# A decoder layer with product-key experts: expert numbers made on chip, sub keys in four loads, list ranks in two-byte numbers, V's gathers tied to chunks, two late loads moved

## The chip, the cores and the metric

One core of a Trainium2 chip runs the whole layer in one launch. TensorE (PE) multiplies, VectorE (DVE) and ScalarE (ACT) work on rows of numbers, GpSimd (POOL) and SyncE (SP) here mostly start transfers (DMAs). Each engine works through its own list of instructions in order, and waits at an instruction until what that needs is there. The metric is the time of one run on the device in microseconds (us), lower is better; times are given as the median of several runs.

## What is computed

A decoder layer on 256 tokens of width 2048 in float32, and a last rmsnorm: two kinds of attention side by side, attention into a memory, and then a layer of experts, in which the change lies (the attention parts are left out here):

```python
def peer_ffn(x, w_q, sub_keys, u_tab, v_tab):      # 8 heads, 128 keys, 16 of the best
    q = (x @ w_q).reshape(T, 8, 2, 128)
    s = einsum('thpd,hpkd->thpk', q, sub_keys)
    top_s, top_i = top_k(s, 16)                    # for each half of the key
    cand = top_s[:, :, 0, :, None] + top_s[:, :, 1, None, :]
    best_s, best_c = top_k(cand, 16)
    expert = ia * 128 + ib                         # one of 16384
    gate = softmax(best_s)
    a = einsum('td,ted->te', x, u_tab[expert])
    return einsum('te,ted->td', gate * gelu(a), v_tab[expert])
h = h + peer_ffn(rmsnorm(h), ...)
y = rmsnorm(h)
```

## The kernel before

PE multiplies in float32 split in two: ACT rounds a block of weights to `hi` (line 75), DVE forms `lo = raw - hi` (line 77), and PE multiplies both, `hi` by 512 columns (line 124) and `lo` by 256 (line 126). SP loads the weights in halves of 512 KB into `raw` (line 66), a ring of four buffers; `hi` and `lo` are rings of three. A wait or a tie ("pin") can be put on any instruction: `pin` fixes only the order on one engine, `behind(ins, n)` makes an instruction wait for the n-th last `lo` that was written, so that it comes "in step with the blocks". Within these ties a list scheduler sets the order of each engine's instructions when the kernel is built.

The expert layer (`peer`) goes through these stages:

- **Queries and sub keys** (about 528 to 600 us). 16 blocks of `w_pq` are multiplied; for each of eight heads a 128 KB piece of the sub keys (`sk`, line 763) is loaded by SP. `whole`, a 2 MB copy of the hidden state, is loaded by POOL (line 758). The choice of the best 16 then goes on in pieces on DVE.
- **U** (about 600 to 1390 us). 128 chunks of U, 1 MB each, are multiplied by all tokens; gelu of each goes to a hidden tile `hb`, one tile for eight chunks, 16 tiles in all (`hidden_tile`). A hidden tile has 258 columns for each chunk: 256 tokens, and two for the number of the expert. The numbers come from a table in HBM, one load for each tile on SP (line 846, `hb<-number`, 128 x 8 x 2 words). In this stage POOL scatters the gates one by one into a `table` (line 1090, 256 indirect DMAs); it is read back and multiplied in.
- **Lists.** Experts that some token chose are sorted into five classes; `lists(part)` is called for experts 0 to 83 of each column (part 0, during U) and 84 to 127 (part 1, when V begins). Its steps `flags`, `totals`, `ranks`, `offsets`, `place`, `spots` are called one at a time between blocks of weights. `totals` and `ranks` are PE products of a matrix of 0 and 1 (`f`) with a triangle (`before`) in float32; `tot`, a copy of the totals, sits in a buffer of the `raw` ring. Then POOL writes the chosen hidden rows, sorted, to HBM (`rows`, line 967).
- **V** (about 1390 to 1710 us). POOL gathers the rows of V that are on a list, 128 rows (1 MB) at a time, 88 times, into the same buffers as the hidden tiles (`fetch`, line 1141, `vrows<-V,index`); the index of a class is loaded ahead (line 1137). PE multiplies with the sorted rows (`listed`), line 1170. The first ten gathers are called one per chunk after part 0's rows are written. `run` calls units of V's work, and every second half block a step of the list of part 1.
- **End.** `v_phase` first loads `res` (hidden state, `fin<-hres`, 2 MB, line 1249) and `gain` (`fin<-norm_final`, 1 MB, line 1250), and `one` (lines 1273 and 1274) is a square root of one element of `gain` that brings ACT's table of square roots in before the last rmsnorm needs it.

Of the kernel before, what the change touches and what calls it, by code (L numbers as in the profile page):

```python
# [18 lines left out]
F32 = mybir.dt.float32  # L19
F32R = mybir.dt.float32r  # L20
U32 = mybir.dt.uint32
# [7 lines left out]
T = 256  # L29
# [24 lines left out]
class Layer:  # L54
    def __init__(self, tc, a):
        self.tc, self.nc, self.a = tc, tc.nc, a
        self.written = ([], [])
        self.spread = {}
        self.pace = []
        self.hold = None  # L60
        self.last_mm = None


# [643 lines left out]
    def peer(self):  # L707
        nc, tc, a = self.nc, self.tc, self.a
        with ExitStack() as es:
# [5 lines left out]
            token = ba.tile([128, 2], F32, name="token")  # L715
            nc.gpsimd.dma_start(token, a["token"])
            self.token = token
            self.listing = False
# [13 lines left out]
            with ExitStack() as e2:  # L732
# [14 lines left out]
                with tc.tile_pool(name="tk", bufs=1, reuse_waits="tile") as tk:  # L747
# [5 lines left out]
                    self.rstd_rows(self.rstd, self.rstd, "sc", 2)  # L753
                    i16 = self.i16 = self.iota[:, :16]
                    whole = tk.tile([128, KD, T], F32, name="whole")
                    for q in range(4):
# [4 lines left out]
                    for h in range(8):  # L761
                        sk = tk.tile([128, 2, 128], F32, tag="sk", name="sk", bufs=8)
                        nc.sync.dma_start(sk, a["subkeys"][:, 2 * h:2 * h + 2, :])
                        if 2 <= h < 6:
                            for _ in range(2):
                                self.hidden_tile(ba)
                        pq = []
                        for p2 in range(2):
                            q = tk.tile([128, T], F32, tag="q", name="q", bufs=16)
                            if (h, p2) == (7, 1):  # L770
                                p = self.whole_block(a["w_pq"][2 * h + p2], whole)
                                nc.scalar.activation(q, p, AF.Copy)
                                self.renew(whole)
                            else:
                                p = self.fm_block(a["w_pq"][2 * h + p2], self.x3)
                                self.join(p, q)
                            pq.append(q)
                            step(2 * h + p2)
                        for tb in range(2):
                            pieces += self.topk_pieces(h, tb, pq, sk)  # L780
# [7 lines left out]
                cl = self.cl = es.enter_context(tc.tile_pool(name="cl", bufs=1, reuse_waits="tile"))  # L788
                self.before = cl.tile([128, 128], F32, name="before")
                nc.gpsimd.dma_start(self.before, a["before"])  # L790
                self.count = cl.tile([128, 2, 128], F32, name="count")
# [9 lines left out]
                while c < 128:  # L801
# [22 lines left out]
                    if part == 1 and not late and len(self.sets) < 10:  # L824
                        self.fetch(len(self.sets))
                    if steps:
                        steps.pop(0)()
# [15 lines left out]
    def hidden_tile(self, pool):  # L843
        t = pool.tile([128, GROUP, W], F32, tag="hb", name="hb", bufs=8)
        g = len(self.buf)
        self.nc.sync.dma_start(t[:, :, T:].bitcast(U32), self.a["number"][:, g * GROUP:(g + 1) * GROUP, :])
        self.buf.append(t)
# [35 lines left out]
    def lists(self, part, pool, tag, bufs):  # L883
# [8 lines left out]
        c = self.count[:, :, lo:hi]  # L892
        f, ok = t("f", 5), t("ok", 4)
        where = cl.tile([128, n], U32, tag="where", name="where")
# [13 lines left out]
        def totals():  # L908
            p = pool.tile([128, 512], F32, tag=tag, name="ps_tot", bufs=bufs)
            for j in range(5):  # L910
                ins = nc.tensor.matmul(p[:n, j:j + 1], f[:, j, :], self.ones[:, :1], start=True, stop=True)
                if j == 0:
                    self.pin(ins, self.last_mm)
            tot = self.st.tile([128, 4 * W], F32, tag="raw", name="tot", bufs=RAW)
            got["tot"] = tot = tot[:, :640].rearrange("p (k e) -> p k e", k=5)
            self.pin(nc.vector.tensor_copy(tot[:n], p[:n, :5].unsqueeze(2).to_broadcast([n, 5, 128])))

        def ranks():
# [4 lines left out]
            for j in range(5):  # L923
                ins = nc.tensor.matmul(got["sum"][:, j:j + 1], tot[:n, j, :], self.ones[:n, :1], start=True, stop=True)
                if j == 0:
                    self.pin(ins, self.last_mm)
                nc.tensor.matmul(p[:, j, :], self.before, f[:, j, :], start=True, stop=False)  # L927
                nc.tensor.matmul(p[:, j, :], tot[:n, j, :], self.before[:n, :n], start=False, stop=True)  # L928

        def offsets():  # L930

            s = small[:, 0:5]
# [23 lines left out]
        def spots():  # L956
            x = f[:, 0]
            self.pin(v.tensor_scalar(x, q, limit, ROWS[part] - limit - base[ALL], op0=ALU.is_ge, op1=ALU.mult))
# [4 lines left out]

        steps = [flags, totals, ranks, offsets, place, spots]

# [165 lines left out]
    def fetch(self, i):  # L1131

        nc = self.nc
        part, cls, k = self.seq[i]
        if (part, cls) not in self.index:
            t = self.cl.tile([128, CAPS[part][cls]], U32, name="index%d%d" % (part, cls))
            ins = nc.gpsimd.dma_start(t.unsqueeze(2), self.listed(part, cls)[:, :, T:T + 1].bitcast(U32))  # L1137
            self.after(ins, part)
            self.index[part, cls] = t
        raw = self.homes[i].tile([128, GROUP * W], F32, tag="hb", name="vrows", bufs=8)[:, :D]  # L1140
# [6 lines left out]
    def v_phase(self):  # L1147
# [6 lines left out]
        with ExitStack() as es:  # L1154
# [5 lines left out]
            def bank(tb):  # L1160
                ps = es.enter_context(psum("vps%d" % tb))
                out.append([ps.tile([128, 512], F32, name="out%d%d" % (tb, q)) for q in range(4)])
# [59 lines left out]
            def run(upto, beside=[], steps=[], every=2):  # L1222


                while at[0] < self.ends[upto]:
# [8 lines left out]
                    for hf in range(2):  # L1234
                        for unit in units:
                            half(unit, hf)
                            turn[0] += 1
                            if turn[0] % every:
                                continue
# [8 lines left out]
            bank(0)  # L1248
            nc.gpsimd.dma_start(res, self.hres)
            nc.gpsimd.dma_start(gain, a["norm_final"].partition_broadcast(128))  # L1250
            with psum("cps") as cps:
# [10 lines left out]
                assert not steps  # L1262
            bank(1)
            run(1, late)

            for tb in range(2):
# [5 lines left out]
            one = vw.tile([128, 1], F32, tag="fy", name="one", bufs=2)  # L1272
            nc.scalar.activation(one, gain[:, :1], AF.Square)
            nc.scalar.activation(one, one, AF.Sqrt)
# [152 lines left out]
def arrays_of(x, mem, t5_table, norm_mix, w_in, cmp_pos_k, cmp_w1_k, cmp_w2_k, cmp_pos_v, cmp_w1_v,  # L1427
# [43 lines left out]
    r["before"] = (i[:, None] < i[None, :]).astype(f)  # L1471
    r["number"] = np.zeros((128, 128, W - T), np.uint32)
    r["number"][:, :, 0] = i[None, :] * 128 + i[:, None]
    r["order"] = (i[None, :] * 128 + i[:, None]).astype(f)
# [18 lines left out]
```

## Time and profile before

| | |
|---|---|
| runs | 1728.80, 1727.91, 1722.69 us; median 1727.91 us |
| the profiled execution | 1721.46 us, of which the span of instructions is 1719.7 us; mean granted clock of TensorE 0.982 |
| busy | PE 1646.6 us (96%), DVE 1260.7 (73%), ACT 1004.6 (58%), POOL 763.0 (44%) |
| moved | 419.08 MB in 137197 packets, 39273 of them under 512 B |
| largest groups | `lo` on DVE 534.7 us, `hi` on ACT 460.2 us, PE's products of line 124 585.5 us and of line 126 323.7 us |

PE is busy for 96% of the span. A busy PE is not PE at its peak: it counts as busy while a product runs at half clock too. So the count of products in a stretch, beside its busy time and its granted clock, says more than the share. PE's busy time by itself leaves 73.1 us of the span.

### The profile page before, as it was taken

How to read it: one execution, taken by the hardware profiler on the slowest of the kernel's cores; microseconds unless marked ns; L12 is line 12 of the kernel's file. 1: busy time of each engine (PE TensorE's matmuls, PEld its weight loads, DVE VectorE, ACT ScalarE, POOL GpSimd, SP SyncE). 2: the span in 40 equal slices, each digit the busy share in tenths (PEclk: the TensorE clock that was granted, in tenths of full speed). 3: DMA queues.
4: the chain of work that ended last, by engine and by line, in shares of the span. 5: the costliest groups of instructions: out<-in, count | busy, mean ns of one | idle time of the engine just before them, and what ended most of it. 6: DMA issues, size and time to landing. Idle time of an engine off the chain costs nothing. (4 is left out here: it accounts for less than half of the span.)

```text
span 1719.7 us, 25752 instructions
## 1 busy us (share of the span) xinstructions
PE 1646.6 (96%) x8808; PEld 1392.2 (81%) x8808; DVE 1260.7 (73%) x2260; ACT 1004.6 (58%) x1486; POOL 763.0 (44%) x652
## 2 busy tenths in 40 slices
PE   8999999999999999999999899999999989899996
PEld 6788777887888888888888688878788766677874
DVE  6875664556768888899999358787556469688687
ACT  7555556765566456566665356654455456567566
POOL 6510000212224376787888741102886216886620
PEclk9999999999999999999999899999999989999998
DMA  8668344889847666566656468766788956998991
GB/s 301 232 213 272 117 163 144 314 313 387 314 136 234 211 187 181 175 195 186 184 174 197 131 191 305 257 232 220 243 277 260 386 214 249 362 402 311 413 406 60
DMA packets 137197, 419.08 MB, mean 244 GB/s; under 512 B 39273, under 2 KB 52201, under 8 KB 123360
## 3 DMA queue, kind: packets, MB, share of 16 engines
q1 hardware_dynamic: 97424, 253.69, 45.5%
q0 software_dynamic: 39344, 163.13, 25.6%
q8 instruction: 71, 1.16, 0.3%
q14 instruction: 70, 0.57, 0.1%
q10 hardware_dynamic: 288, 0.52, 0.1%
HBM read 373.40 MB, written 51.75 MB: 247 GB/s over the span
## 5 line engine op out<-in xcount | busy, mean ns | idle before, releaser
L77 DVE TENSOR_TENSOR lo<-raw,hi 128x1024 fp32r<-128x1024 f32 x433 | 534.7, 1239 | 248.2 <-ACT hi L75 155.5
L75 ACT ACTIVATE hi<-raw 128x1024 fp32r<-128x1024 f32 x437 | 460.2, 1056 | 373.9 <-issue 127.2
L124 PE MATMUL acc<-pair_f,hi 128*128 128x512 f32 x2288 | 585.5, 398 | 14.9 <-ACT hi L75 9.8
L124 PEld LDWEIGHTS acc<-pair_f,hi 128*128 128x128 f32 x2288 | 416.1, 191 | 95.0 <-ACT hi L75 10.6
L1090 POOL DMA_INDIRECT table<-total,place x256 | 328.7, 1284 | 143.3 <-DVE lo L77 62.6
L126 PEld LDWEIGHTS acc<-pair_f,lo 128*128 128x128 f32 x2288 | 314.8, 192 | 33.8 <-issue 6.6
L126 PE MATMUL acc<-pair_f,lo 128*128 128x256 f32 x2288 | 323.7, 284 | 9.2 <-issue 5.6
L967 POOL DMA_INDIRECT rows<-hb,where x128 | 152.0, 1187 | 72.9 <-issue 35.0
L1141 POOL DMA_INDIRECT vrows<-V,index x88 | 124.0, 1410 | 77.3 <-DVE lo L77 21.7
L104 ACT ACTIVATE hi<-vrows,val 128x1024 fp32r<-128x1024 f32 x96 | 109.5, 1148 | 79.5 <-PE out L1170 42.4
L106 DVE SCALAR_TENSOR_TENSOR lo<-vrows,val,hi 128x1024 fp32r<-128x1024 f32 x96 | 123.0, 1283 | 40.2 <-ACT hi L104 32.6
L124 PE MATMUL acc<-pair_x,hi 128*128 128x512 f32 x512 | 132.4, 397 | 0.0
L77 DVE TENSOR_TENSOR lo<-vrows,hi 128x1024 fp32r<-128x1024 f32 x80 | 97.8, 1222 | 13.8 <-issue 4.7
L124 PEld LDWEIGHTS acc<-pair_x,hi 128*128 128x128 f32 x512 | 92.0, 190 | 16.6 <-issue 0.8
L75 ACT ACTIVATE hi<-vrows 128x1024 fp32r<-128x1024 f32 x80 | 84.1, 1052 | 21.4 <-PE out L1170 17.7
L1170 PE MATMUL out<-hi,hh 128*128 128x512 f32 x256 | 82.1, 411 | 14.7 <-ACT hi L75 5.9
L1170 PE MATMUL out<-hi,hl 128*128 128x512 f32 x256 | 82.4, 404 | 0.2
L1170 PE MATMUL out<-lo,hh 128*128 128x512 f32 x256 | 78.3, 407 | 0.6 <-DVE lo L77 0.4
L126 PE MATMUL acc<-pair_x,lo 128*128 128x256 f32 x512 | 75.1, 285 | 0.0
L126 PEld LDWEIGHTS acc<-pair_x,lo 128*128 128x128 f32 x512 | 70.9, 191 | 5.0
L1170 PEld LDWEIGHTS out<-hi,hh 128*128 128x128 f32 x256 | 47.0, 191 | 32.2 <-ACT hi L75 11.8
L124 PE MATMUL acc<-pair_o,hi 128*128 128x512 f32 x256 | 64.8, 394 | 3.8 <-ACT hi L75 2.9
(397 smaller groups left out, 2229.1 us busy)
## 6 DMA issues: line engine op xcount, KB each, us to landing
raw<-U SPq DMA_DIRECT2D x256, 512.0 KB
raw<-w_sb SPq DMA_DIRECT2D x32, 512.0 KB
table<-zero POOLq DMA_DIRECT2D x16, 1024.0 KB
raw<-w_out SPq DMA_DIRECT2D x32, 512.0 KB
raw<-w_pq SPq DMA_DIRECT2D x32, 512.0 KB
listed<-rows SPq DMA_DIRECT2D x88, 129.0 KB
rows<-zero POOLq DMA_DIRECT2D x12, 903.0 KB
gates<-table POOLq DMA_DIRECT2D x20, 512.0 KB
```

The source lines that it names most:

```text
L75: nc.scalar.activation(hi, raw, AF.Copy)
L77: self.last_lo = (eng or nc.vector).tensor_tensor(out=lo, in0=raw, in1=hi.bitcast(F32), op=ALU.subtract)
L104: nc.scalar.activation(hi, raw, AF.Copy, scale=val)
L106: self.last_lo = nc.vector.scalar_tensor_tensor(lo, raw, val, hi.bitcast(F32), op0=ALU.mult, op1=ALU.subtract)
L124: mm(ps, hi[:, n * m:(n + 1) * m], pair[:, k, :], start=first and n == 0, stop=False)
L126: self.last_mm = mm(ps[:, T:], lo[:, n * m:(n + 1) * m], pair[:, k, :T], start=False, stop=last and n == len(ks) - 1)
L967: ins = nc.gpsimd.indirect_dma_start(out=self.rows[part], out_offset=bass.IndirectOffsetOnAxis(ap=where[:, i - lo:i - lo + 1], axis=0), in ...
L1090: ins = self.nc.gpsimd.indirect_dma_start(out=self.table, out_offset=bass.IndirectOffsetOnAxis(ap=self.place[tb][:, s:s + 1], axis=0), in_ ...
L1141: self.gather = nc.gpsimd.indirect_dma_start(out=raw, out_offset=None, in_=self.a["V"], in_offset=bass.IndirectOffsetOnAxis(ap=self.index[ ...
L1170: self.last_mm = mm(out[tb][hf * 2 + q], h, v[:, q * 512:(q + 1) * 512], start=first and n == 0, stop=last and n == len(passes) - 1)
```

## The change

Six parts, of which the core of the diff follows.

1. `hidden_tile` no longer loads the numbers; DVE computes them from a row 0..7 (`iota`) and a small constant `base`, 128 x 16, loaded once.
2. The sub keys come in four loads of 256 KB on POOL's queue, ahead of `whole`, into one tile.
3. `f`, `before`, `tot` and the column of ones are two-byte numbers (BF16), which hold these whole numbers exactly; the five products of `f` with `before` become one of 420 (part 1: 220) columns; `tot` leaves the `raw` ring; `before` is loaded to a buffer of that ring first and cast.
4. `offsets` and `place` are one step, and the steps of part 1's list are called after each half block of V.
5. `fetch` loads the indices of up to three following gathers behind the last gather; each of the first ten gathers waits for the latest `lo` of its chunk.
6. `fin<-hres` is put behind the gathers that `run(0)` calls, `fin<-norm_final` behind those of `run(1)`; `one` goes to the place where it is written, near the end.

```diff
@@ peer
+            self.base = ba.tile([128, 16], F32, name="base")
+            nc.gpsimd.dma_start(self.base, a["base"])
...
+                    keys = tk.tile([128, 16, 128], F32, name="sk")
+                    for q in range(4):
+                        nc.gpsimd.dma_start(keys[:, q * 4:q * 4 + 4, :], a["subkeys"][:, q * 4:q * 4 + 4, :])
                     whole = tk.tile([128, KD, T], F32, name="whole")
...
-                        sk = tk.tile([128, 2, 128], F32, tag="sk", name="sk", bufs=8)
-                        nc.sync.dma_start(sk, a["subkeys"][:, 2 * h:2 * h + 2, :])
+                        sk = keys[:, 2 * h:2 * h + 2, :]
...
-                self.before = cl.tile([128, 128], F32, name="before")
-                nc.gpsimd.dma_start(self.before, a["before"])
+                self.before = cl.tile([128, 128], BF16, name="before")
+                wide = self.st.tile([128, 4 * W], F32, tag="raw", name="wide", bufs=RAW)[:, :128]
+                nc.gpsimd.dma_start(wide, a["before"])
+                self.pin(nc.vector.tensor_copy(self.before, wide))
...
                         self.fetch(len(self.sets))
+                        self.behind(self.gather, 1)
@@ hidden_tile
-        self.nc.sync.dma_start(t[:, :, T:].bitcast(U32), self.a["number"][:, g * GROUP:(g + 1) * GROUP, :])
+        self.pin(self.nc.vector.tensor_scalar(t[:, :, T:].bitcast(U32), self.iota[:, :GROUP].unsqueeze(2).to_broadcast([128, GROUP, W - T]),
+                                              128.0, self.base[:, g:g + 1], op0=ALU.mult, op1=ALU.add))
@@ lists
-            tot = self.st.tile([128, 4 * W], F32, tag="raw", name="tot", bufs=RAW)
+            got["tot"] = tot = wide[:, :320].bitcast(BF16).rearrange("p (k e) -> p k e", k=5)
...
             for j in range(5):
-                ins = nc.tensor.matmul(got["sum"][:, j:j + 1], tot[:n, j, :], self.ones[:n, :1], start=True, stop=True)
+                ins = nc.tensor.matmul(got["sum"][:, j:j + 1], tot[:n, j, :], self.unit[:n, :1], start=True, stop=True)
...
-                nc.tensor.matmul(p[:, j, :], self.before, f[:, j, :], start=True, stop=False)
-                nc.tensor.matmul(p[:, j, :], tot[:n, j, :], self.before[:n, :n], start=False, stop=True)
+            nc.tensor.matmul(p.rearrange("p k e -> p (k e)"), self.before, f.rearrange("p k e -> p (k e)"),
+                             start=True, stop=False)
+            for j in range(5):
+                nc.tensor.matmul(p[:, j, :], tot[:n, j, :], self.before[:n, :n], start=False, stop=j == 4)
...
-        steps = [flags, totals, ranks, offsets, place, spots]
+        steps = [flags, totals, ranks, lambda: (offsets(), place()), spots]
@@ v_phase
+                            if steps and every == 2:
+                                steps.pop(0)()
+                                continue
                             if turn[0] % every:
...
             bank(0)
-            nc.gpsimd.dma_start(res, self.hres)
-            nc.gpsimd.dma_start(gain, a["norm_final"].partition_broadcast(128))
...
             bank(1)
+            self.pin(nc.gpsimd.dma_start(res, self.hres), self.gather)
             run(1, late)
+            self.pin(nc.gpsimd.dma_start(gain, a["norm_final"].partition_broadcast(128)), self.gather)
...
-            nc.scalar.activation(one, gain[:, :1], AF.Square)
+            self.pin(nc.scalar.activation(one, gain[:, :1], AF.Square))
```

How the order of instructions stands, by engine. A row gives the line, the operation, what is written and read, the size, and how often in a row. First SP's queue, from the first weights of the query to the end of U, before the change (`sk` are sub keys, `hb<-number` the numbers of a hidden tile):

```order
L66 DMA raw<-w_pq 128x1024 x8
L763 DMA sk<-subkeys 128x256 x3
L846 DMA hb<-number 128x8x2 x2
L66 DMA raw<-w_pq 128x1024 x2
...
L846 DMA hb<-number 128x8x2 x2
L763 DMA sk<-subkeys 128x256 x2
L66 DMA raw<-w_pq 128x1024 x21
L66 DMA raw<-U 128x1024 x116
L846 DMA hb<-number 128x8x2 x8
L66 DMA raw<-U 128x1024 x140
```

and of the changed kernel, from the memory's weights to V's first sorted rows:

```order
L67 DMA raw<-w_mem_q 128x1024 x8
L67 DMA raw<-w_mem_o 128x1024 x8
L67 DMA raw<-w_pq 128x1024 x32
L67 DMA raw<-U 128x1024 x256
L1205 DMA listed<-rows_80 128x258 x19
```

Nothing is left between SP's loads of weights. Next the load of `before`. It stood on POOL ahead of all puts of gates (`table<-total,place`; `whole` is the copy of the hidden state):

```order
L716 DMA token<-token 128x2
L758 DMA whole<-hres 128x1024 x4
L790 DMA before<-before 128x128
L1090 DMA table<-total_4916,place_4918 4194304x1 x16
L1090 DMA table<-total_4917,place_4919 4194304x1 x16
```

It now goes to a buffer of the `raw` ring (`wide`), and on POOL it stands behind the first 194 of the 256 puts; the sub keys stand ahead of `whole`:

```order
L717 DMA token<-token 128x2
L719 DMA base<-base 128x16
L760 DMA sk<-subkeys 128x512 x4
L764 DMA whole<-hres 128x1024 x4
L1102 DMA table<-total_4916,place_4918 4194304x1 x16
...
L1102 DMA table<-total_4916,place_4918 4194304x1 x2
L796 DMA wide<-before 128x128
L1102 DMA table<-total_4916,place_4918 4194304x1 x14
```

and on DVE, among the pieces of the last choice of experts (`bs`, `bi`, `place`), the cast that reads it:

```order
L997 MAX bs<-cand 128x8
L78 TENSOR_TENSOR lo<-raw,hi 128x1024
L799 CAST unit<-ones 128x2
L797 CAST before<-wide 128x128
L1064 TENSOR_SCALAR place_4918<-key,token 128x16
L998 MAX_INDEX bi<-bs,cand 128x8
L1000 MATCH_REPLACE rest<-bs,cand 128x256
L1037 TENSOR_SCALAR bm<-bs 128x1
L78 TENSOR_TENSOR lo<-raw,hi 128x1024
```

The cast stands behind the 277th `lo<-raw,hi` of the kernel, counted in DVE's order; the last eight hidden tiles' numbers (line 856) are written on DVE behind the 290th and the 291st. Last ACT around `one`, before, among the first blocks of V (`hh` is the rounded part of the sorted rows):

```order
L104 ACTIVATE hi<-vrows,val 128x1024
L75 ACTIVATE hi<-vrows 128x1024
L1273 ACTIVATE one<-fin 128x1
L1274 ACT_TABLE_LOAD
L1274 ACTIVATE one<-one 128x1
L1177 ACTIVATE hh<-listed 128x128 x2
L104 ACTIVATE hi<-vrows,val 128x1024
```

and in the changed kernel, among the last blocks of V and the squares of the last rmsnorm (line 1300):

```order
L1300 ACTIVATE fin,z_17103<-out_14370 128x512
L1291 ACTIVATE one<-fin 128x1
L1192 ACTIVATE hh<-listed 128x128
L105 ACTIVATE hi<-vrows,val 128x1024
L76 ACTIVATE hi<-vrows 128x1024
L1292 ACT_TABLE_LOAD
L1292 ACTIVATE one<-one 128x1
L105 ACTIVATE hi<-vrows,val 128x1024
L1300 ACTIVATE fin,z_17103<-out_14371 128x512
```

The table of square roots is now loaded in the last stage instead of the first of V. On POOL, `fin<-hres` and `fin<-norm_final` stood right behind the tenth gather; now the first stands ahead of the twelve writes (line 979) that begin part 1's rows, and the second 70 rows behind it, past part 1's index loads. On DVE the last step of part 1's list (`where`) stands behind the same `lo` of V, the 23rd, in both kernels.

More of the change, by code (lines that the diff above doesn't have):

```diff
@@ L61, in __init__ @@
         self.last_mm = None
+        self.gather = None
     def raw(self, src):
@@ L788, in peer @@
                 cl = self.cl = es.enter_context(tc.tile_pool(name="cl", bufs=1, reuse_waits="tile"))
-                self.before = cl.tile([128, 128], F32, name="before")
-                nc.gpsimd.dma_start(self.before, a["before"])
+                self.before = cl.tile([128, 128], BF16, name="before")
+                wide = self.st.tile([128, 4 * W], F32, tag="raw", name="wide", bufs=RAW)[:, :128]
+                nc.gpsimd.dma_start(wide, a["before"])
+                self.pin(nc.vector.tensor_copy(self.before, wide))
+                self.unit = cl.tile([128, 2], BF16, name="unit")
+                self.pin(nc.vector.tensor_copy(self.unit, self.ones[:, :2]))
                 self.count = cl.tile([128, 2, 128], F32, name="count")
@@ L892, in lists @@
         c = self.count[:, :, lo:hi]
-        f, ok = t("f", 5), t("ok", 4)
+        f, x = cl.tile([128, 5, n], BF16, tag="f", name="f"), cl.tile([128, n], F32, tag="x", name="x")
+        wide = cl.tile([128, 336], F32, tag="ok", name="ok")
+        ok = wide[:, :4 * n].rearrange("p (k e) -> p k e", k=4)
         where = cl.tile([128, n], U32, tag="where", name="where")
@@ L910, in totals @@
             for j in range(5):
-                ins = nc.tensor.matmul(p[:n, j:j + 1], f[:, j, :], self.ones[:, :1], start=True, stop=True)
+                ins = nc.tensor.matmul(p[:n, j:j + 1], f[:, j, :], self.unit[:, :1], start=True, stop=True)
                 if j == 0:
                     self.pin(ins, self.last_mm)
-            tot = self.st.tile([128, 4 * W], F32, tag="raw", name="tot", bufs=RAW)
-            got["tot"] = tot = tot[:, :640].rearrange("p (k e) -> p k e", k=5)
+            got["tot"] = tot = wide[:, :320].bitcast(BF16).rearrange("p (k e) -> p k e", k=5)
             self.pin(nc.vector.tensor_copy(tot[:n], p[:n, :5].unsqueeze(2).to_broadcast([n, 5, 128])))
@@ L956, in spots @@
         def spots():
-            x = f[:, 0]
             self.pin(v.tensor_scalar(x, q, limit, ROWS[part] - limit - base[ALL], op0=ALU.is_ge, op1=ALU.mult))
@@ L1133, in fetch @@
         nc = self.nc
-        part, cls, k = self.seq[i]
[L1135 to L1139, printed above, removed]
+        for p, cls, _ in self.seq[i:i + 3]:
+            if (p, cls) not in self.index and p == self.seq[i][0]:
+                t = self.cl.tile([128, CAPS[p][cls]], U32, name="index%d%d" % (p, cls))
+                ins = nc.gpsimd.dma_start(t.unsqueeze(2), self.listed(p, cls)[:, :, T:T + 1].bitcast(U32))
+                self.after(ins, p)
+                if self.gather is not None:
+                    self.pin(ins, self.gather)
+                self.index[p, cls] = t
+        part, cls, k = self.seq[i]
         raw = self.homes[i].tile([128, GROUP * W], F32, tag="hb", name="vrows", bufs=8)[:, :D]
@@ L1471, in arrays_of @@
     r["before"] = (i[:, None] < i[None, :]).astype(f)
-    r["number"] = np.zeros((128, 128, W - T), np.uint32)
-    r["number"][:, :, 0] = i[None, :] * 128 + i[:, None]
+    r["base"] = (np.arange(16)[None, :] * (GROUP * 128) + i[:, None]).astype(f)
     r["order"] = (i[None, :] * 128 + i[:, None]).astype(f)
```

## The prediction

> **What bounds the kernel now.** The engine table comes first: PE is busy for nearly the whole span.
>
> ```profile
> PE 1646.6 (96%) x8808; PEld 1392.2 (81%) x8808; DVE 1260.7 (73%) x2260; ACT 1004.6 (58%) x1486; POOL 763.0 (44%) x652
> ```
>
> A stage can then only get shorter where PE does fewer products in a time than it can, or does products that go away. So the second view is PE's busy time by stretch, with the count of products; the stretches lie where the change touches the work, the first and the fifth where nothing disturbs U and V, the last inside the second.
>
> ```profile
> core 0: us, PE busy (x), PEclk, DMA share, GB/s
> 900.00:936.00 36.00, 36.00 (x208) 1.00 0.61 190
> 942.00:978.00 36.00, 27.67 (x118) 0.76 0.49 115
> 556.00:576.00 20.00, 16.53 (x91) 0.91 0.74 223
> 1348.00:1364.00 16.00, 12.49 (x63) 0.89 1.01 419
> 1612.00:1668.00 56.00, 56.00 (x242) 1.00 1.02 414
> 1389.00:1445.00 56.00, 45.39 (x176) 0.85 0.77 293
> 954.00:972.00 18.00, 9.67 (x27) 0.63 0.23 78
> ```
>
> An undisturbed product of U costs 36/208 = 0.173 us, one of V 56/242 = 0.231 us. 942 to 978 is 90 products short: 15.6 us. 556 to 576 should hold 116 and holds 91: 4.3 us. 1348 to 1364 should hold 92.5 and holds 63: 5.1 us. Of the 176 records at V's opening 40 belong to the lists, so 136 of 242 are V's: 24.5 us. That is what there is to win, 49.5 us; the rest of the kernel is at its rate.
>
> **The numbers of the experts.** SP's timeline at the hole in U, the transfers of 943 to 952, and one of PE's waits in 942 to 978:
>
> ```profile
> 941.03 7.71 SPq L846 DMA_DIRECT2D hb<-number  x8
> 948.84 35.04 SPq L66 DMA_DIRECT2D raw<-U  x10
> ```
>
> ```profile
> DMA packets 8594, 0.33 MB, mean 36 GB/s; under 512 B 8531, under 2 KB 8531, under 8 KB 8594
> ```
>
> ```profile
> PE acc L126 <- issue: 4.7, 6, 1.1
> ```
>
> The eight loads hold SP for 7.71 us, and their 8531 packets leave 36 GB/s, where U takes 190 GB/s. The loads go; on DVE eight small writes of 16 elements come, at some 0.2 us each (the smallest operation of ACT below takes 0.20), and 8 KB of `base`: 1.6 us, hidden by the microseconds that a `lo` lies ready before PE takes it up (4.2 us in the next part); without that cover it is 1.6 us. I take the whole 15.6 us. The lower end is little above 0: PE is slowest from 954 to 972, after the packets, and waits there for nothing that the profile shows (the issue row). The other eight loads and the sub keys lie between `w_pq` loads, and ACT waits for these (waits of 541 to 571):
>
> ```profile
> ACT hi L75 <- DMA raw<-w_pq: 8.3, 2, 6.4
> ```
>
> 4 us of 4.3. The sub keys, 1 MB, now go ahead of `whole` on POOL's queue: at 190 GB/s 5.5 us, behind which `whole` lands later; ACT scales `whole` one or two `hi` later than before, which covers about that. Bounds: 0 and 5.
>
> **The cast of `before`: a new wait.** The load stood before all puts; now it stands behind 194 of them, and DVE waits for it in its own order. Where DVE comes to it, where POOL then is, and where PE is (timelines; the first POOL row is an undisturbed put, the one of 917.78 the 195th, the last a gather that waits for a small load of POOL):
>
> ```profile
> 907.62 1.21 DVE L77 TENSOR_TENSOR lo<-raw,hi 128x1024 fp32r<-128x1024 f32 x1
> ...
> 910.86 2.03 DVE L1063 TENSOR_TENSOR dup<-place 128x1792 f32<-128x1792 uint32 x1
> ```
>
> ```profile
> 904.14 0.98 POOL L1090 DMA_INDIRECT table<-total,place  x1 [0.30 <-issue]
> ...
> 909.99 3.75 POOL L1090 DMA_INDIRECT table<-total,place  x1 [0.30 <-DVE bm L1025]
> 914.05 3.42 POOL L1090 DMA_INDIRECT table<-total,place  x1 [0.31 <-DMA table<-total,place]
> 917.78 1.23 POOL L1090 DMA_INDIRECT table<-total,place  x1 [0.30 <-issue]
> ...
> 1336.00 1.04 POOL L1141 DMA_INDIRECT vrows<-V,index  x1 [2.19 <-DMA index<-rows]
> ```
>
> ```profile
> 915.12 1.11 PE L126 MATMUL acc<-pair_f,lo 128*128 128x256 f32 x8
> ```
>
> The 277th `lo` is that of 907.62; it ends at 908.8, and there is the cast. POOL works without a pause, so the load is issued when the 194th put ends, at 917.5 by these rows; with some 2.5 us to its landing (estimate from the gather's wait of 2.19 us, which is the last part of such a landing) DVE stands still for 11 us. If the two long puts are long because of DVE's work beside them (`dup` lies inside the first), a still DVE lets them take 0.98 us: the load is issued at 912.3, and DVE waits 6 us. Behind the cast stand pieces of the choice and the next `lo`, which was done at 910.95 and which PE took up at 915.12, 4.2 us later; of the following eleven, counted in the same way, the closest has 1.9 us to spare, and DVE has no idle time before 940 in which to catch up. PE so loses 4 to 9 us, and up to 1.7 more by half clock: ends 4 and 11. I take 6, since the long puts stand just where DVE is busy. The Trainium skill ("SBUF — State Buffer", Who interferes with whom) speaks against that: it infers that DVE's tensor_tensor, which `dup` is, does not keep POOL from writing descriptors. By it the puts stay long, the cast costs 9 to 11, and the sum below is 4 us higher; the row of 3.75 us lies beside `dup` and so leans against it, without proof.
>
> **The ranks.** PE's groups of part 0's ranks, and the first and last of part 1's 30 records:
>
> ```profile
> L927 PE MATMUL ps_rank<-f,before 128*128 128x84 f32 x10 | 2.2, 297 | 0.0
> L928 PE MATMUL ps_rank<-before,tot 84*128 84x84 f32 x10 | 1.9, 275 | 0.0
> L924 PE MATMUL ps_rank<-ones,tot 84*128 84x1 f32 x10 | 1.6, 224 | 0.0
> ```
>
> ```profile
> 1408.78 0.38 PE L924 MATMUL ps_rank<-ones,tot 44*128 44x1 f32 x2
> ...
> 1413.15 0.65 PE L928 MATMUL ps_rank<-before,tot 44*128 44x44 f32 x2
> ```
>
> Each product in float32 is two passes. Part 1: 30 records from 1408.78 to 1413.8, 5.0 us (0.165 each), now ten of one pass and a wide one (0.3, estimate from 297 ns for 84 columns of these): 2.0, so 3.0 us saved. Part 0, whose 30 records are busy for 5.7 us and overlap to 3.3: by the same shares 2.0 saved, and half a microsecond more for both totals: 5.5. Bounds 0 (a pass in two bytes could cost what two cost) and 8 (all of it).
>
> **The burst of gathers.** Transfers of 1338 to 1348, by queue (POOL's, then SP's):
>
> ```profile
> q0 software_dynamic: 401, 2.92, 70.0%
> q1 hardware_dynamic: 350, 1.29, 31.9%
> ```
>
> U gets 1.29 MB in 10 us, 129 GB/s. One gather for each chunk takes 3.6 us at POOL's 292 GB/s, in a chunk of 5.55 us (32 products); U moves 0.46 MB beside it and 0.8 MB in the rest at 414 GB/s, where it needs 1.05. So the burst's loss goes: 4.5 of 5.1 (0 to 5.1).
>
> **V's opening.** ACT, PE's next product, and one behind a later wait; then two stretches at half clock:
>
> ```profile
> 1400.75 0.20 ACT L1273 ACTIVATE one<-fin 128x1 f32<-128x1 f32 x1 [3.67 <-DMA fin<-norm_final]
> 1400.97 1.28 ACT L1274 ACT_TABLE_LOAD   x1
> ```
>
> ```profile
> 1402.71 1.22 PE L1170 MATMUL out<-hi,hh 128*128 128x512 f32 x2 [3.91 <-ACT hh L1177]
> ```
>
> ```profile
> 1439.84 0.63 PE L1170 MATMUL out<-hi,hh 128*128 128x512 f32 x1 [2.57 <-DVE total L951]
> ```
>
> ```profile
> 1412.70:1419.50 6.80, 6.80 (x18) 0.50 0.92 329
> 1440.00:1443.40 3.40, 3.40 (x9) 0.50 1.02 421
> ```
>
> ACT waits in order for `gain`, then loads the table, and `hh` is behind both: 3.91 us, and 1.7 for the half clock after it. With part 1's ranks cut to 2 us I let the 6.8 us at half clock behind them go as well (3.4). With 5.6 and 3.4 this is 9.0. The clock also halves after 2.57 us of waiting (the stretch at 1440, which stays, behind `place`). The Trainium skill ("TensorE: Matmul & The Clock Gate", Part 1: The HAM clock gate) halves it only after an idle window of about 3.4 us; by that rule the 6.8 us, with no gap ahead of them, have a cause that the change leaves, and the sum is 3.4 us higher; the row of 1440 speaks against the rule.
>
> Costs: `offsets` with `place` in one step puts about 1 us more of DVE work ahead of a `lo` that PE waits for at 1437; the table load of 1.28 us comes where ACT has no idle time (row below): 1.3 us. `hres` and `gain`, 3 MB, move to stretches of V; at 414 GB/s 7.3 us of transfers, hidden by the gathers' lead if that holds, else up to 2 us a megabyte. Earlier calls of the list's steps gain nothing: `where` stands behind the same `lo`.
>
> ```profile
> 1690.00:1700.00 10.00, 10.00 (x17) 1.00 0.01 2
> ```
>
> **Sum.** 15.6 + 4 + 5.5 + 4.5 + 9.0 = 38.6 gained, 6 + 1 + 1.3 = 8.3 lost: 30.3 us. 1721.5 (the profiled run) becomes 1691.2. The three runs have their median 6.4 above that run; I add half of it: 1694.
>
> **Rivals.**
> 1. The slow stretch of 954 to 972 has another cause than the loads and stays. There 27 products stand where 104 fit: 13.3 us not won, 1707. For it: its waits have no releaser, and the packets are over by 953. Against: U's own transfers stand at 78 GB/s there, so its chain of buffers is broken as well.
> 2. The tied gathers starve U all the same: at 129 GB/s a chunk takes 8.1 us instead of 5.55, ten chunks 26 us, 1720. Against: each gather is alone in its chunk.
> 3. The clock rule above: 1698.
> 4. Slower: the wait at the cast grows, DVE standing for POOL's queue. PE's loss is the wait less 1.9 us, so from 38.6 - 2.3 + 1.9 = 38 us on nothing is gained, and at 55 us it is 1727.9 + 17 = 1745. POOL would have to be at its 194th put at 945 instead of 917; it is late by 9 us now, and puts go on to 1014.
>
> **Chances.** Forecast 0.58, rival 1 0.18, 2 0.09, 3 0.09, 4 0.03, and 0.03 for what I don't see. The range takes the cast's ends (1692 to 1700), rival 1 and a better case without the 3.2 us of median, the burst and the table in full (1683): 1682 to 1710; rival 2 and 4 are left out. Within 0.5% (8.6 us, about what a measurement of this kernel tells from no change) is 1719 to 1737, most of it rival 2's upper half: 0.06; slower 0.04; faster 0.9.
>
> **What would show it.** After: no thin stretch behind the 290th `lo`, PE at 208 products in 36 us there; DVE idle 6 to 11 us ahead of a cast of `before` that waits for its load, with a PE gap of some us behind it; no `hb<-number`; ten gathers 5.5 us apart and no gap of PE at 1354; V's first 56 us with about 60 more products; ranks in about 2 us. The prediction is wrong if the thin stretch stays, if a gather delays `hi`, or if DVE stands over 12 us at the cast.

## The result, and the profile after

The changed kernel takes 1714.82 us (median; 1702.78 to 1721.1), the kernel before 1728.3 us beside it: ratio 0.9924, interval 0.9903 to 0.9945. That is faster by 13.5 us, where 34 were forecast; 1714.8 lies above the range of 1682 to 1710. The profiled execution took 1713.96 us, span 1711.9, 7.8 us less than the span before.

The engine table after, and PE's busy time in stretches (columns: from and to, length, PE busy and its instructions, granted clock, DMA share, GB/s):

```profile
PE 1635.5 (96%) x8760; PEld 1378.7 (81%) x8760; DVE 1264.4 (74%) x2278; ACT 1004.4 (59%) x1486; POOL 756.9 (44%) x657
```

```profile
core 0: us, PE busy (x), PEclk, DMA share, GB/s
900.00:936.00 36.00, 33.25 (x187) 1.00 0.62 192
942.00:978.00 36.00, 34.40 (x197) 1.00 0.63 177
970.00:990.00 20.00, 13.65 (x58) 0.84 0.32 89
1208.00:1240.00 32.00, 23.48 (x99) 0.89 0.57 177
...
1382.00:1438.00 56.00, 43.92 (x177) 0.91 0.76 283
1612.00:1668.00 56.00, 56.00 (x241) 1.00 1.02 408
556.00:576.00 20.00, 20.00 (x117) 1.00 0.62 206
```

The queries are whole (117 products, 91 before), and 942 to 978 holds 197 of 208. But 970 to 990 lacks 58 of 116, and 1208 to 1240 lacks 86 of 185. The kernel before had a shortage there too, a small one:

```profile
1208.00:1240.00 32.00, 29.64 (x162) 1.00 0.73 240
```

So the thin stretch did not go; it stands elsewhere, and is longer. PE's rows inside it (start, duration, in brackets the idle time ahead):

```profile
976.41 0.28 PE L127 MATMUL acc<-pair_f,lo 128*128 128x256 f32 x1 [0.69 <-issue]
976.52 0.41 PE L125 MATMUL acc<-pair_f,hi 128*128 128x512 f32 x1
977.84 0.62 PE L125 MATMUL acc<-pair_f,hi 128*128 128x512 f32 x2 [0.92 <-issue]
979.25 1.30 PE L125 MATMUL acc<-pair_f,hi 128*128 128x512 f32 x5 [0.79 <-issue]
```

PE waits again for nothing that the profile shows. With PE's products (the lists' left out) matched one to one by their place in its order, the two kernels' start times give what each stretch gained. The right column is the same for a pair of runs on another chip, told of below:

| stretch, in us of the kernel before | forecast | gained here | gained on the other chip |
|---|---|---|---|
| queries, 559 to 581 | +4 | +4.8 | +2.4 |
| cast, 905 to 928 | -6 | -3.6 | see next row |
| 928 to 1014: thin stretch gone, another come | +15.6 | +15.6, -9.9 | +3.7 (907 to 1019) |
| 1014 to 1142 | 0 | -3.1 | -0.4 (1019 to 1109) |
| totals and ranks of part 0 | +2.5 | +8 | +7.8 |
| thin stretch of 1208 to 1243 | 0 | +3, -14.2 | 0 |
| burst of gathers | +4.5 | +5.3 | +4.2 |
| V's opening, with part 1's ranks | +12 | +11.5 | -5.6, +8.6 |
| wait behind it | -1 | -5.4 | -5.2 |
| the rest | -1.3 | -4.3 | -0.5 |
| sum | +30.3 | +7.7 | +15 |

### The profile page after: what moved, and what is told of

Read it like the earlier page. It is cut to its first block, busy times and chain, and to the rows that moved or that the text cites. A ratio compares the mean times of both kernels' runs of the same rounds, so it can differ in the third digit from the quotient of the medians.

```text
span 1711.9 us, 25653 instructions
## 1 busy us (share of the span) xinstructions
PE 1635.5 (96%) x8760; PEld 1378.7 (81%) x8760; DVE 1264.4 (74%) x2278; ACT 1004.4 (59%) x1486; POOL 756.9 (44%) x657
## 4 chain that ended last, share of the span: by engine, by line
PE 80%; DMA 8%; DVE 5%; issue 4%; ACT 2%; POOL 1%; SPq 0%; DVEq 0%; POOLq 0%; ACTq 0%
PE acc L125 39%; PE acc L127 20%; PE out L1185 11%; DMA gates<-table 3%; DMA vrows<-V,index 2%; PE acc L179 2%; PE acc L185 2%; PE acc L180 2%; DVE lo L78 1%; DMA listed<-rows 1%; ACT hi L76 1%; DMA memT<-memT 1%; DVE hb L825 1%; PE ps_l L603 1%; PE ps_po L617 1%
## 5 line engine op out<-in xcount | busy, mean ns | idle before, releaser
L1185 PE MATMUL out<-hi,hh 128*128 128x512 f32 x256 | 81.9, 408 | 14.7 <-DVE total L964 6.6
```

What stands on the lines that cost most here:

```text
L1185: self.last_mm = mm(out[tb][hf * 2 + q], h, v[:, q * 512:(q + 1) * 512], start=first and n == 0, stop=last and n == len(passes) - 1)
```

## The experiments

### Are the number loads the cause of the thin stretches?

Four kernels on one chip. `e1_numbers` is the kernel before with part 1 alone (DVE forms `base` there instead of a load); `e2_sp_numbers` is the changed kernel without part 1:

```diff
-        self.pin(self.nc.vector.tensor_scalar(t[:, :, T:].bitcast(U32), ..., self.base[:, g:g + 1], op0=ALU.mult, op1=ALU.add))
+        self.nc.sync.dma_start(t[:, :, T:].bitcast(U32), self.a["number"][:, g * GROUP:(g + 1) * GROUP, :])
```

> The kernel before, with part 1 alone: the experts' numbers are written by DVE (from iota and the token column), and SP's 16 loads of numbers are gone. Theory A (thin stretches of PE, where it issues one instruction in some 0.7 us and waits for nothing shown, come with POOL's scattered writes and not from the number loads): the profile still has thin stretches of 10 to 25 us in all between 900 and 1250, the median is 4 to 8 us under before. Rival B (the loads made the one at 954): U runs at 0.173 us a product from 600 to 1100 but for the waits known, and the median is 14 to 20 us under before.

> The changed kernel with part 1 undone: SP loads the numbers again, the rest as changed. Theory A: within 6 us of the changed kernel (1709 to 1721), lost only what the 7.7 us of SP's issue cost at 941 and in the queries; thin stretches of the same sum as in the changed kernel. Rival B: 14 to 20 us slower than the changed kernel, 1729 to 1735, with a thin stretch right behind the loads.

Measured against 1729.73 us: e1 1726.33 (0.9989, interval 0.9968 to 1.001), e2 1726.74 (0.9972, 0.9953 to 0.9992). Part 1 alone gains nothing there that can be told from zero. PE's stretch in e1, which has no number loads at all:

```profile
900.00:990.00 90.00, 84.09 (x443) 0.92 0.56 169
```

443 products where 520 fit (208 in 36 us). The hole stays without the loads, so they aren't its cause.

e2 fits neither of its theories: it lies 8 to 11 us above e3 and e4 (told of next, on the same chip), more than A's 6 us over the changed kernel, and below B's 1729. Its thin stretches are longer in its profile (sums below), and the queries lack some 28 of 116 products, near 5 us. But PE keeps its full rate while the eight loads run (SP is at them from 956.24 to 963.91); the stretch at 972 to 984 comes later, at a place where the changed kernel, without loads, has one too:

```profile
960.00:972.00 12.00, 12.00 (x69) 1.00 0.76 170
972.00:984.00 12.00, 9.01 (x35) 0.72 0.55 167
```

`e3_res_late` starts `fin<-hres` only behind the first write of part 1's rows; `e4_cast` loads `before` early to a tile of its own:

```diff
+                                if len(beside) == 44 - 1:
+                                    self.pin(nc.gpsimd.dma_start(res, self.hres), ins)
-            self.pin(nc.gpsimd.dma_start(res, self.hres), self.gather)
```

```diff
+            wide = ba.tile([128, 128], F32, name="wide")
+            nc.gpsimd.dma_start(wide, a["before"])
-                wide = self.st.tile([128, 4 * W], F32, tag="raw", name="wide", bufs=RAW)[:, :128]
-                nc.gpsimd.dma_start(wide, a["before"])
```

> The changed kernel with the load of res (2 MB) behind the first write of part 1's rows instead of ahead of the last gather of V's opening. Theory (at 1417 this load fills the queue beside the gathers, listed lands late, DVE waits 3.4 us for it ahead of the list's place, and PE stands for 6.6 us at 1420): that gap of PE is 2 to 3 us, as before the change, and the time 4 to 6 us shorter than the changed kernel's. Rival (the joined offsets and place block makes the gap, whatever res does): the gap stays 5 us or more, the time within 2 us.

> The changed kernel with before loaded ahead of the sub keys into a tile of its own, so that the cast on DVE finds it there and no raw buffer is taken. Theory (the cast's wait for POOL's queue costs PE 3 to 4 us in gaps at 910, 915 and 918): these gaps go, the time is 3 to 4 us shorter. Rival (PE's gaps there are DVE's own load of work and would come anyway): gaps stay, time within 1.5 us.

e3 1718.56 (0.9922, 0.9897 to 0.9947), e4 1715.55 (0.9898, 0.9877 to 0.9919). Both intervals overlap the changed kernel's, so neither gain that was expected (4 to 6 and 3 to 4 us) is seen. In e4 DVE waits for nothing at the cast, but a thin stretch stands near its place, and shows its beat best:

```profile
904.07 0.37 PE L127 MATMUL acc<-pair_f,lo 128*128 128x256 f32 x1 [0.34 <-issue]
904.80 0.37 PE L127 MATMUL acc<-pair_f,lo 128*128 128x256 f32 x1 [0.35 <-issue]
905.52 0.37 PE L127 MATMUL acc<-pair_f,lo 128*128 128x256 f32 x1 [0.35 <-issue]
906.24 0.40 PE L127 MATMUL acc<-pair_f,lo 128*128 128x256 f32 x2 [0.34 <-issue]
```

One product each 0.72 us, with no releaser. Summed between 600 and 1380 us, and estimated from the products that are short of the undisturbed rate, the thin stretches cost about 20 us in the kernel before, 26 in the changed one, 19 in e1, 35 in e2, 28 in e3 and 29 in e4, each in one profile.

### The same kernels on other chips

`e5_fewer` and `e5_again` leave out half of the puts of gates and three of four row writes of part 0, to see whether POOL's transfers make the stretches; their gates and rows are incomplete, so their times are no gains. The others repeat kernels of above.

> The changed kernel without the puts of gates of heads 4 to 7 (128 of 256 are left out) and with every fourth of part 0's row writes only (21 of 84): the gates and rows are then not complete; only the stage of U, from 780 to 1330, is read. Theory A (the thin stretches come with POOL's scattered writes): no thin stretch at 970 to 990 and none, or under 4 us in all, at 1205 to 1240. Rival C (they belong to a place in PE's own instructions): 5 to 11 us at 970 to 990 and 15 to 19 us at 1205 to 1240 as in the changed kernel.

> The kernel before, profiled once more. If the thin stretches are a state of the chip and not of the kernel: either the same two places again (some 15 us behind 950, 4 at 1215) on a chip that shows them, or none in U, and then no loss behind the number loads beyond what the loads themselves keep from U (4 to 8 us).

> The changed kernel, profiled once more beside the kernel before. On a chip without thin stretches: 14 to 22 us shorter than before (ratio 0.987 to 0.992), as the kernels with the small mends were; on one with them: 10 to 16 us, thin stretches of 25 us again at 975 and 1207.

> The kernel before with part 1 alone, as in the first such run. Rival B would have 14 us or more under before whatever the chip; theory A 2 to 8 us, all of it where SP's loads of numbers stood.

> The changed kernel with SP's loads of numbers again, as in the first such run. If the numbers cost what they keep from SP and the queues: 5 to 12 us slower than the changed kernel on this chip, seen at 540 to 580 and at 920 to 960 and nowhere else; if only thin stretches made the first run slow, within 3 us where there are none.

> The changed kernel once more, as the standard for the next runs on the same chip: 12 to 22 us under before, by whether the chip shows thin stretches in U.

> As the run with fewer puts and writes (half the puts, a quarter of part 0's row writes; gates and rows are not complete, and only U is read). On a chip whose other kernels show thin stretches: none here by theory A, the same as theirs by rival C. On a chip without them it tells nothing new.

On four further chips the kernel before takes 1709.0 to 1710.8 us, some 19 less, and none of the 14 profiles taken there shows a thin stretch. With the products of the same kernel matched between two chips, the stretches have a price that needs no such estimate, in one profile each: the kernel before loses 15.6 us at 954 to 978 and 4.0 at 1208 to 1243 against `b_again`, the changed one 9.9 at 968 to 992 and 15.2 at 1205 to 1240 against `a_again`. That is 19.6 and 25.1 us; the whole profiles differ by 13.5 and 20.7, since other places go the other way.

So e5 (1676.82 us, ratio 0.9807, 0.9769 to 0.9845, and 1682.4 in one run) met no thin stretch, and what makes them stays open. The two long ones stand beside POOL's puts of gates (954 to 978) and its row writes (1205 to 1240), but the same puts and writes run on the four chips without any, so by themselves they are not enough. `b_again` gave 1710.59 (1.0004, 0.9982 to 1.0027), `a_again` 1689.53 (0.9875, 0.9844 to 0.9905), `a_third` 1692.69 (0.9896, 0.9871 to 0.9921), `e1_again` 1705.15 (0.9973, 0.9952 to 0.9995) and `e2_again` 1697.59 (0.9926, 0.99 to 0.9952). The kernel before took 1710.76 us beside these, a_third apart (1709.72). Part 1 is worth 5.6 us alone there (1710.76 - 1705.15) and 8.1 as the last part (1697.59 - 1689.53). Not from the place of the hole: in `b_again`, the kernel before, eight number loads hold SP for 8.73 us and PE loses nothing.

```profile
937.88 8.73 SPq L846 DMA_DIRECT2D hb<-number  x8
```

```profile
942.00:978.00 36.00, 36.00 (x208) 1.00 0.72 199
```

Most of the 8.1 comes from the eight loads among the queries: matched, `a_again` gains 6.2 us there on `e2_again`, and 9.1 in the whole profile. Of the 5.6, the profiles show 2.6 at that place. PE there in `e2_again`, then in `a_again`:

```profile
556.00:576.00 20.00, 16.33 (x86) 0.91 0.60 183
```

```profile
556.00:576.00 20.00, 20.00 (x118) 1.00 0.68 227
```

### The totals' buffer and the tie

`e6_tot_raw` puts `tot` back into the ring of U, still in two bytes. `e7_untied` lets the first ten gathers go at will, `e11_tie5` ties each to a `lo` two chunks earlier. e11 is not the changed kernel with that edit alone, as its expectation has it: it also has the two edits of `e10_steps_cast` below, so what it is measured against is `e10_again`, on the same chip. The diffs of e6, e7, and of e11 against e10:

```diff
-            got["tot"] = tot = wide[:, :320].bitcast(BF16).rearrange(...)
+            tot = self.st.tile([128, 4 * W], F32, tag="raw", name="tot", bufs=RAW)
+            got["tot"] = tot = tot[:, :320].bitcast(BF16).rearrange(...)
```

```diff
-                        self.behind(self.gather, 1)
```

```diff
-                        self.behind(self.gather, 1)
+                        self.behind(self.gather, 5)
```

> The changed kernel with tot in a buffer of the raw ring again, still as two-byte numbers. Theory (tot in the ring held up U's loads; the gap of 2.85 us at 1160 with its half clock went because tot left the ring): the gap is back, 3 to 5 us slower than the changed kernel. Rival (the two-byte products alone shortened that place): time as the changed kernel within 2 us, no gap there.

> The changed kernel without the tie of the first ten gathers to chunks. Theory (the burst of gathers starves U): PE's gap of some 3.5 us and the half clock at 1350 are back, 4 to 6 us slower than the changed kernel. Rival (the index loads ahead spread the gathers by themselves): within 2 us.

> The changed kernel with the first ten gathers of V tied to the fifth last lo instead of the last (two chunks earlier); nothing else. Theory A (the untied run's: gathers put off by the tie are the transfers that stand in the full queue when part 0's sorted rows are read, so that DVE and PE wait some 7 us at 1401 to 1408): the gathers start at most 11 us earlier, the burst's loss at 1312 to 1356 stays under 3 us, and PE's gap at 1401 falls from 7.3 us to between 3 and 6; on a chip where the kernel before takes 1710 us, 1 to 4 us less than the changed kernel's 1690 to 1693. Theory B (the gap is part 1's list itself, independent of when gathers run): gap 7 us as before, time within 1 us of the changed kernel's.

e6 1691.68 us (0.9897, 0.9869 to 0.9924), e7 1695.44 (0.9921, 0.9892 to 0.9949), e11 1690.32 (0.9885, 0.9843 to 0.9926). PE behind the totals in e6, in `a_again` and in `b_again`:

```profile
1145.82 3.78 PE L125 MATMUL acc<-pair_f,hi 128*128 128x512 f32 x8 [3.75 <-ACT hi L76]
```

```profile
1147.54 2.09 PE L125 MATMUL acc<-pair_f,hi 128*128 128x512 f32 x8
```

```profile
1149.94 2.64 PE L124 MATMUL acc<-pair_f,hi 128*128 128x512 f32 x8 [2.85 <-ACT hi L75]
```

With `tot` in the ring, PE waits 3.75 us for `hi` and then runs eight products in 3.78 instead of 2.09 us; without it there is no wait. So the buffer, more than the width of the numbers, is what this stage paid for: matched against e7, on the same chip and without `tot` in the ring, e6 loses 7 us by 1154. In the medians it is about 2 us at most, and the intervals overlap. Matched against `a_again`, on another chip without thin stretches, e6 is 6.7 us behind at 1154 and level with it at 1364: there, what the changed kernel wins at the totals is lost again ahead of V, where the last chunks of U land beside the gathers.

PE's wait in V's opening, in `a_again`, in e7, in `e10_again` and in e11:

```profile
1408.47 0.76 PE L1185 MATMUL out<-hi,hh 128*128 128x512 f32 x1 [7.27 <-DVE total L964]
```

```profile
1318.71 2.73 PE L125 MATMUL acc<-pair_f,hi 128*128 128x512 f32 x8 [2.38 <-ACT hi L76]
...
1405.00 0.48 PE L1184 MATMUL out<-hi,hh 128*128 128x512 f32 x1 [3.04 <-DVE total L963]
```

```profile
1402.32 0.76 PE L1185 MATMUL out<-hi,hh 128*128 128x512 f32 x1 [7.73 <-DVE total L964]
```

```profile
1408.52 0.77 PE L1185 MATMUL out<-hi,hh 128*128 128x512 f32 x1 [8.30 <-DVE total L964]
```

Untied, the burst starves U again (8 us against `a_again` between 1312 and 1345), and the wait falls from 7.27 to 3.04. But 6.7 of the 8 us are made up by 1372, ahead of that wait, as in e6, and in the whole profile e7 is 1.9 us shorter than `a_again`. Its median is 3 to 6 us above the changed kernel's on two other chips, with intervals that overlap, so what the tie is worth in the time is not shown.

Two chunks earlier does not help. Against `e10_again` the last three of the ten gathers start 6.5 to 13 us earlier, U loses some 6 us more between 1339 and 1355, where theory A allowed 3, and the wait stays, as B had it. The median is 2 us above `e10_again`'s 1688.16, and the intervals overlap.

### Joined steps, and a version to keep

`e8_both` is e3 and e4 together, `e9_steps` undoes part 4, and `e10_steps_cast` is e9 with e4's load:

```diff
-        steps = [flags, totals, ranks, lambda: (offsets(), place()), spots]
+        steps = [flags, totals, ranks, offsets, place, spots]
...
-                            if steps and every == 2:
-                                steps.pop(0)()
-                                continue
```

> The changed kernel with before loaded early into a tile of its own and res behind the first write of part 1's rows. If both costs are separate and go: gaps at 910 to 920 and at 1420 are gone in the profile, and by the profiles 8 to 10 us are won; if the thin stretches of U take up what is won ahead of them, the median is only 0 to 4 us under the changed kernel's.

> The changed kernel with part 4 undone: offsets and place are two steps again and one step is called for every second half block, as before. Theory (the joined block makes the gap of 6.6 to 7.3 us in V's opening, because on DVE it now stands right behind two takings of val from listed, the second of which waits for its load, and PE waits for the lo behind the block): the gap is 1 to 3.5 us, 4 to 5 us shorter than the changed kernel at that place, 2 to 4 us in the time. Rival (the gathers that the tie makes later fill the queue there, and listed lands late whatever the order): the gap stays 5 us or more.

> Part 4 undone, and before loaded early into a tile of its own: the best version that the runs so far point to. 3 to 7 us under the changed kernel if the gap in V's opening goes, within 2 us of it if not.

> The changed kernel with offsets and place as two steps again and the constant before loaded early to a tile of its own; a second run of the best version so far. Theory A (the joined step is worth its 3 to 6 us, whatever the chip): ratio to the kernel before 0.984 to 0.988. Theory B (the earlier ratio of 0.986 was a lucky pair): 0.989 to 0.992, as for the changed kernel.

e8 1691.96 (0.9888, 0.9856 to 0.9919; its wait in V's opening is 6.94 us, so the gap that was to go stays), e9 1685.9 (0.986, 0.9841 to 0.9879), e10 1686.44 (0.9864, 0.9844 to 0.9883), and again 1688.16 (0.9876, 0.9833 to 0.9918). Beside e9 and e10, on the same chip, the changed kernel took 1692.69. PE's wait in V's opening is 6.94 us in e9 and 7.37 in e10, so the joined step doesn't make it. e9 and e10 have the lowest medians of all the complete kernels, 6 to 7 us below the changed one; the repeat's interval holds the changed kernel's ratio too, so the gain is likely and not shown.

## Why the prediction was wrong

**The numbers: the step that failed.** "I take the whole 15.6 us." The prediction put PE's hole of 942 to 978 down to the number loads, because these stand on SP just ahead of it. e1 has no such loads and has the hole; `b_again` has the loads and no hole. It was rival 1 that held, a thin stretch of another cause; it gave 1707, with a chance of 0.18, and even that was too good, because the thin stretches are not just kept but some 6 us longer in all. The prediction had the evidence: its own rows said "issue" as the releaser, and the packets were over at 953. While the loads ran, PE was at its full rate in the kernel before, too:

```profile
941.00:954.00 13.00, 13.00 (x77) 1.00 0.69 104
```

U's 78 GB/s in the hole, used against the rival, fits a PE that takes little: the changed kernel's hole, with no such load near, has 89 GB/s. That 8.7 us of these loads cost PE nothing in `b_again` also says how much the chunks that lie ready cover.

**Queries: right**, 4 forecast, 4.8 and 2.4 measured.

**The cast: right mechanism, price too high.** POOL's load and DVE's wait, then PE's three waits behind them, from the changed kernel on the result's chip:

```profile
906.89 0.60 POOL L796 DMA_DIRECT2D wide<-before  x1
```

```profile
  DMA wide<-before: 5.5, 1
```

```profile
911.54 1.22 PE L127 MATMUL acc<-pair_f,lo 128*128 128x256 f32 x8 [1.66 <-DVE lo L78]
...
915.27 1.21 PE L127 MATMUL acc<-pair_f,lo 128*128 128x256 f32 x8 [0.67 <-issue]
...
918.74 1.21 PE L127 MATMUL acc<-pair_f,lo 128*128 128x256 f32 x8 [0.42 <-DVE lo L78]
```

DVE waits 5.5 us (6 to 11 forecast), PE 2.75 in the three waits and 3.6 in all. That is the prediction's own rule, the wait less 1.9 us; the price was too high because the wait was shorter. The load was issued at 906.89, not at 912 or later, since POOL came earlier to its 194th put; long puts (1.94, 1.96 and 3.10 us) still stand beside `dup`, behind the load. So the term was not decided by the rule on the shared memory that was weighed there ("SBUF — State Buffer" of the Trainium skill, Who interferes with whom): no run took `dup` away. On the other chip the wait was 2.1 us and PE lost none, which the rule gives as well (0.2).

**Ranks: the reason was incomplete.** Of the 5.5, 2.5 belonged to part 0. Measured are 8, most of it the wait for `hi` that `tot` in the ring caused; the prediction listed that `tot` leaves the ring and priced only the products. The products got as short as forecast: the two wide ones take 303 ns in the mean (338 for 420 columns, 268 for 220).

```profile
L939 PE MATMUL ps_rank<-f,before 128*128 128x420 bf16 (+1 forms) x2 | 0.6, 303 | 0.0
```

**The burst: right in size here, wrong in picture.** 5.3 and 4.2 us for 4.5; on the other chip 5.6 us are lost right behind it. And the gathers did not stand 5.5 us apart: the lists' rows came late, so four went almost at once, and the rest as the ties allowed. POOL's first, fourth, fifth and last:

```profile
1323.75 1.07 POOL L1156 DMA_INDIRECT vrows<-V,index  x1 [1.89 <-DVE count L890]
...
1331.54 1.00 POOL L1156 DMA_INDIRECT vrows<-V,index  x1 [0.85 <-DVE lo L78]
1337.13 1.00 POOL L1156 DMA_INDIRECT vrows<-V,index  x1 [4.59 <-DVE lo L78]
...
1365.07 1.03 POOL L1156 DMA_INDIRECT vrows<-V,index  x1 [2.37 <-DVE lo L78]
```

**V's opening: right as a sum; what follows it was mis-sized.** 11.5 us for 12 on the result's chip. No run takes part 6 back alone, so how much of it the moved loads and how much the shorter ranks gave is not shown. But "about 1 us" for DVE's work behind it became 5.4. The waits of 1414 to 1430 in the changed kernel:

```profile
PE out L1185 <- DVE total L964: 6.6, 1, 6.6
DVE val L1211 <- DMA listed<-rows: 3.4, 2, 2.4
```

DVE stands for two sorted rows, then does the small pieces of `place` in its order, and the next `lo` comes behind both. The rows come late where the queue is full: 8.2 us from issue to landing between 1376 and 1412 in `a_again`, 3.9 between 1342 and 1358, at 358 and 268 GB/s:

```profile
listed<-rows SPq DMA_DIRECT2D x9, 129.0 KB, 8.2
```

```profile
listed<-rows SPq DMA_DIRECT2D x6, 129.0 KB, 3.9
```

The untied run and e9 speak against the list's steps alone and point to the order of transfers; that is argued, not shown, and e11, whose gathers start earlier too, does not bear it out. Which transfer it is was not found: moving `hres` behind the wait left 5.7 us in e3:

```profile
1429.40 0.76 PE L1185 MATMUL out<-hi,hh 128*128 128x512 f32 x1 [5.70 <-DVE total L964]
```

On the other chip 5.6 us are also lost ahead of V, where the last chunks of U land beside gathers and sorted rows.

**The clock.** Stretches behind the wait of 6.6 us (changed kernel) and behind that of 2.38 us, which ends at 1318.71 (e7):

```profile
1426.00:1431.00 5.00, 4.26 (x11) 0.53 0.89 373
```

```profile
1318.70:1320.00 1.30, 1.29 (x6) 0.99 0.96 394
1320.00:1322.00 2.00, 2.00 (x8) 0.50 1.06 438
```

The clock is near half in the first once PE starts again, and half in the second 1.3 us later; e7's eight products of 1318.71 take 2.73 us, where `a_again`'s at full clock take 2.09. The rule that the clock halves only after about 3.4 us ("TensorE: Matmul & The Clock Gate" of the Trainium skill, Part 1: The HAM clock gate) fits the first and not the second, and here the measurement decides. Rival 3 did not decide the time.

**Rivals 2 and 4** did not come: U was not starved by the tied gathers in the profile here (5.6 us were lost on the other chip, not 26), and the cast cost under 4 us. The tail (1.3 forecast) cost 1.6 to 1.7.

Without the 15.6 of the numbers the sum is 14.7. On the chips without thin stretches 17.0 to 21.2 were gained in the medians and 15 in the profiles: the rest of the working held as a sum, in part by luck, since its errors cancel (ranks +5.5, wait behind the opening -4.4).

## What to carry to other kernels

A hole behind a transfer isn't that transfer's: when the starved engine's waits name no releaser and the transfer is over before the hole begins, price it as not won, and try the removal alone. When a tile leaves a ring of stream buffers, price the wait that it caused there ahead of the shorter work, and ask whether a later stage takes it back. Bursts that are spread out can come due later: ask which small loads stand behind them in the queue. Repeat the pair of kernels on another chip before a hole is put down to the code.

## What the runs showed of the hardware

The same program differs by some 19 us between chips (1729 and 1710 us): on the slower ones PE at times issues one product each 0.72 us for 5 to 30 us, with no wait that the profile shows, at places that move with the code. The cause is open. Half clock for some microseconds follows waits of PE as short as 2.4 us (granted clock 0.50 over 1320 to 1322 in e7).
